# Five edits to the token mixing of a decoder block: gating's product on another engine, three projection tiles at once, the norm's end in single tiles, triangles turned later

## The chip, the core and the metric

The kernel runs on one core of a Trainium2 chip, in one launch. The metric is the device time in microseconds; a run's time is that of its one core. Three runs of the kernel before took 1669.92 to 1671.87 us, with a median of 1670.35.

## What is computed

The reference is one layer of a hybrid decoder block on 1024 positions of width 1024, all in float32. It has three parts, each with an RMS norm before and after it and a residual:

- token mixing: h = norm(x), then one projection of h gives u and v (1024 columns each, GELU), the input of a diagonal state-space branch S5 (512) and two gates (1024 each);
- attention into a memory of 256 positions;
- a SwiGLU network with 2816 hidden columns.

The change is in the token mixing, and in the norm of the memory at the start. What matters of it, cut from the reference:

```python
y   = rms_norm(mem, g_mem)                                 # 256 x 1024, at the kernel's start
u, v = split(gelu(z_gm)); v = layer_norm(v)
w   = where(tril, w_s, 0)                                  # 8 triangles of 128 x 128
sv  = einsum('gts,bnsgc->bntgc', w, v) + b_s               # per chunk of 128 positions
y_gm = u * sv                                              # the gating
y_s5 = y * sigmoid(y @ w_glu)                              # end of S5, 512 channels
merged = sigmoid(z_ga) * (y_gm @ w_br_gm) + sigmoid(z_gb) * (y_s5 @ w_br_s5)
```

## The kernel before, in words

**Precision.** Each operand of a large product is split into a high half (a cast to fp32r on ScalarE) and a low half (the rest, a subtraction on VectorE), and each product is three matmuls of halves (`mm3`, L521; the matmuls themselves show as L519). `put` (L527 to 530) makes such a split: the cast at L529, the subtraction at L530. Weights are loaded by SyncE's queue (`load`, L89) into three raw buffers and split into pairs (`split`, L98: cast L103, subtraction L104); SyncE asks for the next load as soon as the subtraction has freed a raw buffer. There are eight buffers of split weights and eight PSUM banks of 128x512.

**Order of the work.** The order is written out by hand: each engine runs its instructions in the order in which the program issues them, and the queue of an engine stands at an instruction that waits. Work beside the main products is put into generators by `bg(gen, delay)` (L64). `sub()` (L67) counts one turn, runs each generator that is due up to its next `yield n` (due again n turns later), in the order in which they were queued, and then lets `pump` split one weight block ahead if there is room. The product functions call `sub` once or twice to a block: `tblock` (L539) after every second of its four inner steps, `run` in `v_phase` after two of four tiles. `drain` (L79) runs the turns that are left with no matmuls between them.

**The start** (`start`, L649 on). The two memory tiles `ms` are squared and summed on ScalarE, VectorE makes the reciprocal root, `pump` splits the first weight block, then ScalarE scales the first tile (L667) and VectorE the second (L668). Then both are turned on TensorE (`turn`, L582).

**v and the norm** (`v_phase`, L1146 on). v's eight tiles of 128 positions come from products with the operands "11", "T1", ... "T4" in two sets of four banks, X and Y. `ln(half)` (L1153) is the layer norm of four tiles: four squares, one to a turn, VectorE's short operations for the reciprocal root, and at L1165 to 1170 four ACTIVATEs that apply it, two to a turn. `ln(1)` runs beside the product "21", `ln(0)` is queued after "T4" and runs beside the first blocks of `s5_out`. `wturn` (L1218) turns the eight triangles of w_s in two steps of four, each into a bank that ScalarE copies out (L1223, L1224), and then makes in two more steps the bias term, which VectorE adds to `bb`. It is queued after VectorE's sums out of the banks Y, ahead of "T4".

**S5's output** (`s5_out`, L1060 on). Four glu tiles, each in two halves: product, sigmoid on ScalarE (L1076), product on VectorE, split. Then the projection by channels to 1024 columns: eight blocks `m` of two halves, each times the gate read back from DRAM (`gb`). Blocks 0 and 1 are done at once in four banks: first the inner steps 0 to 2 of all four tiles, nine matmuls each, then the last step of all four. That way the fourth glu tile is wanted later. Blocks 2 to 7 follow one by one, twelve matmuls a half.

**The gating** (`gm_gen`, L1259 on) is queued ahead of the projection with a delay of 3 and runs beside it: 16 steps (8 groups, two halves), one every second turn. A step is eight short matmuls, VectorE's scale and bias out of the bank (stt), the product with u (`self.tt`, u loaded from DRAM by SyncE one group ahead, L1267), and `put` for the split that the merge multiplies with. `merge` (L1291 on) begins with `drain`; its first block takes the low and high halves of the eight groups in turn.

Of the kernel before, what the change touches and what calls it, by code (L numbers as in the profile page):

```python
# [14 lines left out]
ALU = mybir.AluOpType  # L15
# [21 lines left out]
class Builder:  # L37
# [480 lines left out]
    def mm(self, ps, a, b, start, stop, more=False):  # L518
        self.nc.tensor.matmul(ps, a, b, start=start, stop=stop, skip_group_check=more)  # L519
# [129 lines left out]
    def start(self):  # L649

        nc, i = self.nc, self.ins
        mem, x = i["mem"][0], i["x"][0]
        self.kvd = self.dr.tile([4, P, 1024], F, name="kvd", tag="kvd")
        ms = [self.slot() for _ in range(2)]
        for t, m in enumerate(ms):
            nc.sync.dma_start(m, mem[t * 128:t * 128 + 128])
        self.consts()
        self.load()
        xs = [self.slot() for _ in range(8)]
        lx = lambda half: [nc.sync.dma_start(xs[t], x[t * 128:t * 128 + 128]) for t in range(4 * half, 4 * half + 4)]  # L660
        lx(0)
        st = self.newst()
        for t, m in enumerate(ms):
            self.square(m, st[:, t:t + 1])
        r = self.rms(st, 2)
        self.pump()
        nc.scalar.mul(ms[0], ms[0], r[:, 0:1])  # L667
        self.ts(ms[1], ms[1], r[:, 1:2], ALU.mult)  # L668
        mt = [self.pair(), self.pair()]
        mv = lambda k: tuple(s[:, (k % 4) * 256:(k % 4) * 256 + 256] for s in mt[k // 4])  # L670
        for _ in self.turn(ms, 3, mv):
            pass
        ms = None
        self.hT = [self.pair() for _ in range(8)]
        hs = self.hs = lambda half: lambda k: tuple(s[:, half * 512:half * 512 + 512] for s in self.hT[k])

        def xgen():
            for half in range(2):
                st = self.newst()
                for t in range(4):  # L680
                    self.square(xs[4 * half + t], st[:, t:t + 1])
                    yield 1
                if not half:
                    lx(1)
                r = self.rms(st, 4)
                for t in range(4):
                    self.ts(xs[4 * half + t], xs[4 * half + t], r[:, t:t + 1], ALU.mult)
                yield 4
                yield from self.turn(xs[4 * half:4 * half + 4], 0, hs(half))
                for t in range(4):  # L690
                    xs[4 * half + t] = None
            self.xok = True
            self.s5_load()
            self.bg(self.s5_gen(), 5)
            self.bg(self.h_sums(), 8)
        self.bg(xgen())
        for c in range(2):
            ks = self.slot()
            for m in range(4 * c, 4 * c + 4):
                if m % 2 == 0:  # L700
                    ps = self.bank()
                w = self.get(("k", m))
                self.tblock(ps[:, (m % 2) * 256:(m % 2) * 256 + 256], w, 0, mv, every=4)
                self.rel()
                if m % 2:
                    nc.scalar.copy(ks[:, (m % 4 - 1) * 256:(m % 4 + 1) * 256], ps)
            nc.scalar.dma_start(self.kvd[c], ks)
        vs = [self.slot(), self.slot()]
        for cb in range(2):
            pss = [self.bank(), self.bank()]  # L710
            for kp in range(4):
                w = self.get(("kv", cb, kp))
                self.nblock(pss, w, 2 * kp, lambda k, t: tuple(s[:, t * 128:t * 128 + 128] for s in mv(k)), kp == 3)
                self.rel()
            for t in range(2):
                nc.scalar.copy(vs[t][:, cb * 512:cb * 512 + 512], pss[t])
        for t in range(2):
            nc.scalar.dma_start(self.kvd[2 + t], vs[t])
# [341 lines left out]
    def s5_out(self):  # L1060
        nc = self.nc
        while len(self.yT) < 4 or not self.yok:
            self.sub()
        yT, self.yT = self.yT, None
        yr, self.yr = self.yr, None
        ys = []
        for m in range(4):
            if m % 2 == 0:
                w = self.get(("glu", m // 2))
            y = self.pair()  # L1070
            t = self.slot()
            for half in range(2):
                o = slice(half * 512, half * 512 + 512)
                ps = self.bank()
                self.tblock(ps, w, (m % 2) * 128, lambda k: tuple(s[:, o] for s in yT[k]), 4)
                nc.scalar.activation(out=t[:, o], in_=ps, func=AF.Sigmoid)  # L1076
                self.tt(t[:, o], t[:, o], yr[m][:, o], ALU.mult)
                self.put(tuple(s[:, o] for s in y), t[:, o])
            ys.append(y)
            if m % 2:  # L1080
                self.rel()
        yT = yr = None
        gb = {}

        def lg(m):
            gb[m] = self.slot()
            nc.sync.dma_start(gb[m], self.gd["gb"][m])
        lg(0)
        lg(1)
        self.bg(self.gm_gen(), 3)  # L1090
        late = []
        w = self.get(("bs", 0))

        tiles = [(m, half, self.bank()) for m in range(2) for half in range(2)]
        for ks in (range(3), range(3, 4)):
            for m, half, ps in tiles:
                for k in ks:
                    self.mm3(ps, tuple(x[:, k, m * 128:m * 128 + 128] for x in w),
                             tuple(s[:, half * 512:half * 512 + 512] for s in ys[k]), k == 0, k == 3)
                self.sub()  # L1100
                if ks[0]:
                    o = slice(half * 512, half * 512 + 512)
                    self.tt(gb[m][:, o], ps, gb[m][:, o], ALU.mult)
        tiles = ps = None
        self.rel()
        late += [(self.gd["mb"][m], gb.pop(m)) for m in range(2)]
        lg(2)
        for m in range(2, 8):
            if m < 7:
                lg(m + 1)  # L1110
            if m % 2 == 0:
                w = self.get(("bs", m // 2))
            g = gb.pop(m)
            for half in range(2):
                o = slice(half * 512, half * 512 + 512)
                ps = self.bank()
                self.tblock(ps, w, (m % 2) * 128, lambda k: tuple(s[:, o] for s in ys[k]), 4)
                self.tt(g[:, o], ps, g[:, o], ALU.mult)
            if m % 2:
                self.rel()  # L1120
            while late:
                nc.scalar.dma_start(*late.pop(0))
            late.append((self.gd["mb"][m], g))
        nc.scalar.dma_start(*late.pop(0))
# [21 lines left out]
    def v_phase(self, fin):  # L1146

        nc, i = self.nc, self.ins
# [4 lines left out]
        def ln(half):  # L1153
            st = sums[half]
            mu = st[:, 40:44]
            self.tt(mu, st[:, 32:36], st[:, 36:40], ALU.add)
            self.ts(mu, mu, -1.0 / D, ALU.mult)
            for t in range(4):
                j = self.jk.tile([P, 1024], BF, name="jk", tag="jk", bufs=1)
                nc.scalar.activation(out=j, in_=vt[4 * half + t], func=AF.Square, bias=mu[:, t:t + 1],  # L1160
                                     accum_out=st[:, t:t + 1])
                yield 1
            yield from self.rms_slow(st, 4)
            self.tt(st[:, 48:52], mu, st[:, 16:20], ALU.mult)
            for t in range(4):  # L1165
                v = vt[4 * half + t]
                nc.scalar.activation(out=v, in_=v, func=AF.Identity, scale=st[:, 16 + t:17 + t], bias=st[:, 48 + t:49 + t])  # L1167
                if t % 2:
                    yield 1
            if not half:  # L1170
                self.vok = True
        X, Y = ([self.bank() for _ in range(4)] for _ in range(2))
# [37 lines left out]
        w = self.slot()  # L1210
# [36 lines left out]
            self.tt(vt[t][:, h0], Y[t], vt[t][:, h0], ALU.add)  # L1247
            gelu(vt[t][:, h0], vt[t][:, h0], st(0, 0, t))
        Y = None
        self.bg(wturn(), 2)  # L1250
        run(X, "T4", False)
        del self.fxs["T4"]
        self.hT = None
# [5 lines left out]
    def gm_gen(self):  # L1259
        nc, i = self.nc, self.ins  # L1260
# [10 lines left out]
        for g in range(8):  # L1271
            y = self.pair()
            lu(g + 1)
            u = us.pop(g)
            for half in range(2):
                o = slice(half * 512, half * 512 + 512)
                ps = self.bank()
                for n in range(4):
                    self.mm(ps[:, n * 128:n * 128 + 128], self.vt[4 * half + n][:, g * 128:g * 128 + 128],
                            self.wt[:, g * 128:g * 128 + 128], True, True)  # L1280
                t = self.tmp()
                self.stt(t.rearrange("p (n t) -> p n t", n=4), ps.rearrange("p (n t) -> p n t", n=4), self.gc[:, 32 + g:33 + g],
                         self.bb[:, g * 128:g * 128 + 128].unsqueeze(1).to_broadcast([P, 4, 128]), ALU.mult, ALU.add)
                self.tt(u[:, o], t, u[:, o], ALU.mult)
                self.put(tuple(s[:, o] for s in y), u[:, o])
                yield 2
            self.ygm[g] = y
            u = y = t = ps = None
# [675 lines left out]
```

## Time and profile before

| what | value |
|---|---|
| median of three runs | 1670.35 us |
| the profiled execution's own time | 1670.15 us |
| its span in the profile | 1668.4 us |
| mean granted clock of TensorE | 0.994 |
| busy: TensorE, VectorE, ScalarE, GpSimd | 1628.1, 1150.6, 681.7, 102.7 us |

The span is what the profile shows from the first to the last instruction; about 1.75 us of the execution's time lie around it. A busy TensorE is not TensorE at its peak, since matmuls are pipelined, but a wait of TensorE shows as a gap. In a timeline, the bracket at the end of a row is the idle time of that engine just before the instruction and what ended it. The granted clock of a stretch is given as a share of 2.4 GHz.

### The profile page before, as it was taken

The numbers are of one execution on the slowest core, as the hardware profiler recorded it, in microseconds if no ns is written. First come the engines' busy times: TensorE is split into PE (matmuls) and PEld (weight loads), VectorE is DVE, ScalarE is ACT, GpSimd is POOL, SyncE is SP. The second block draws the span as 40 slices with busy tenths as digits, with TensorE's granted clock in tenths as the row PEclk, the third lists the DMA queues.
The fourth block names the chain that finished last, engine by engine and source line by source line (L and its number), as shares of the span: only waits on it lengthen the run. The fifth ranks groups of instructions, "written<-read, shape, count | busy, mean of one in ns | idle before, by whom it ended". The sixth has DMA issues, their size and how long they took to land.

```text
span 1668.4 us, 20995 instructions
## 1 busy us (share of the span) xinstructions
PE 1628.1 (98%) x7788; PEld 1364.4 (82%) x7788; DVE 1150.6 (69%) x2053; ACT 681.7 (41%) x1196; POOL 102.7 (6%) x97
## 2 busy tenths in 40 slices
PE   7999989999999999999999999999999999999997
PEld 7898878887887778888888888888888888888886
DVE  5679788967444674447864577687778777666778
ACT  6642212135457222235543447753233223245454
POOL 0025500012500000000000000000000000000000
PEclk9999999999999999999999999999999999999999
DMA  8669922245231474444523153673545446463634
GB/s 278 207 122 200 234 74 90 76 134 186 113 113 51 163 283 158 141 147 143 172 69 125 53 192 112 216 244 130 180 139 173 149 158 202 142 225 132 226 112 161
DMA packets 223414, 259.53 MB, mean 156 GB/s; under 512 B 14824, under 2 KB 157200, under 8 KB 223120
## 3 DMA queue, kind: packets, MB, share of 16 engines
q1 hardware_dynamic: 176208, 181.24, 33.7%
q10 hardware_dynamic: 26496, 60.18, 9.7%
q0 software_dynamic: 20608, 16.78, 5.9%
q8 instruction: 61, 1.00, 0.2%
q14 instruction: 41, 0.34, 0.1%
HBM read 183.31 MB, written 77.33 MB: 156 GB/s over the span
## 4 chain that ended last, share of the span: by engine, by line
PE 83%; DVE 7%; ACT 5%; issue 2%; DMA 2%; SPq 0%; ACTq 0%; DVEq 0%
PE ps L519 79%; DVE act L134 2%; DVE ws L104 1%; ACT jk L575 1%; DVE ws L134 1%; ACT ws L103 1%; DMA wr<-in_ca_w_kv_dram 1%; ACT act L529 1%; DVE act L530 1%; DVE act L140 1%; PE ps L587 1%; ACT jk L1160 1%; DMA wr<-actd 1%; PE ps L508 1%; ACT act L1167 0%
## 5 line engine op out<-in xcount | busy, mean ns | idle before, releaser
L519 PE MATMUL ps<-act,ws 128*128 128x512 f32 (+1 forms) x4212 | 970.1, 388 | 9.6 <-ACT act L529 7.3
L519 PEld LDWEIGHTS ps<-act,ws 128*128 128x128 f32 x4212 | 775.4, 189 | 165.9 <-ACT act L529 8.1
L519 PE MATMUL ps<-ws,act 128*128 128x512 f32 x1392 | 332.8, 395 | 0.0
L519 PEld LDWEIGHTS ps<-ws,act 128*128 128x128 f32 x1392 | 270.2, 208 | 45.0
L134 DVE TENSOR_TENSOR act<-act 128x512 f32<-128x512 f32 (+6 forms) x521 | 287.3, 580 | 15.2 <-ACT act L1076 8.0
L519 PE MATMUL ps<-ws 128*128 128x512 f32 x852 | 193.3, 389 | 0.0
L519 PEld LDWEIGHTS ps<-ws 128*128 128x128 f32 x852 | 159.9, 188 | 33.2
L104 DVE TENSOR_TENSOR ws<-wr,ws 128x1024 fp32r<-128x1024 f32 x100 | 122.1, 1223 | 93.3 <-ACT ws L103 93.1
L134 DVE TENSOR_TENSOR act<-ps,act 128x512 f32<-128x512 f32 x201 | 135.6, 683 | 43.5 <-PE ps L519 34.1
L134 DVE TENSOR_TENSOR ws<-act,ws 128x512 fp32r<-128x512 f32 x107 | 74.0, 692 | 88.9 <-ACT ws L1754 51.8
L134 DVE TENSOR_TENSOR ws<-tm,ws 128x512 fp32r<-128x512 f32 x108 | 78.2, 724 | 79.4 <-ACT ws L1547 58.9
L1547 ACT CAST ws<-tm 128x512 fp32r<-128x512 f32 x88 | 54.8, 622 | 168.8 <-PE ps L519 111.5
L103 ACT CAST ws<-wr 128x1024 fp32r<-128x1024 f32 x100 | 104.7, 1047 | 42.8 <-PE ps L519 29.3
L134 DVE TENSOR_TENSOR ws<-wr,ws 128x512 fp32r<-128x512 f32 x130 | 91.7, 706 | 28.2 <-ACT ws L1547 14.9
L529 ACT CAST act<-act 128x512 fp32r<-128x512 f32 (+1 forms) x92 | 57.5, 637 | 129.5 <-DVE act L134 117.1
L530 DVE TENSOR_TENSOR act<-act 128x512 fp32r<-128x512 f32 (+1 forms) x92 | 65.3, 720 | 46.1 <-ACT act L529 46.1
L519 PE MATMUL ps<-act 128*128 128x256 f32 (+2 forms) x504 | 86.6, 317 | 0.2
L519 PEld LDWEIGHTS ps<-act 128*128 128x128 f32 x504 | 74.7, 190 | 9.6 <-DVE act L134 0.8
L1754 ACT CAST ws<-act 128x512 fp32r<-128x512 f32 x71 | 44.2, 622 | 89.6 <-PE ps L519 48.3
L1831 POOL DMA_DIRECT2D out_dram<-act x4 | 2.2, 561 | 1171.8 <-DVE act L134 1171.8
L530 DVE TENSOR_TENSOR act<-ps,act 128x512 fp32r<-128x512 f32 x48 | 32.5, 687 | 39.7 <-ACT act L529 39.7
L890 ACT ACTIVATE act<-ps 128x512 f32<-128x512 f32 x32 | 19.2, 600 | 80.4 <-PE ps L519 46.6
(164 smaller groups left out, 1112.5 us busy)
## 6 DMA issues: line engine op xcount, KB each, us to landing
wr<-in_ffn_w_gu_dram SPq DMA_DIRECT2D x39, 512.0 KB, 4.2
actd<-act ACTq DMA_DIRECT2D x77, 256.0 KB, 2.2
wr<-actd SPq DMA_DIRECT2D x38, 512.0 KB, 3.7
wr<-in_w_in_dram SPq DMA_DIRECT2D x28, 512.0 KB, 3.9
act<-in_ffn_w_gu_dram SPq DMA_DIRECT2D x22, 512.0 KB, 5.1
act<-in_ffn_w_down_dram SPq DMA_DIRECT2D x44, 256.0 KB, 4.3
td<-act POOLq DMA_DIRECT2D x40, 256.0 KB, 6.6
pd<-act ACTq DMA_DIRECT2D x17, 512.0 KB, 4.4
```

What stands on the lines that cost most here:

```text
L103: self.nc.scalar.copy(hi, t)
L104: self.nc.vector.tensor_tensor(out=lo, in0=t, in1=hi.bitcast(F), op=ALU.subtract)
L134: self.nc.vector.tensor_tensor(out=out, in0=a, in1=b, op=op)
L140: self.nc.vector.scalar_tensor_tensor(out=out, in0=a, scalar=s, in1=b, op0=op0, op1=op1)
L508: nc.tensor.matmul(py[:, o], self.rr[:, 512 + i * 128:640 + i * 128], cc[:, 512 + i * 128:640 + i * 128], start=False, stop=True)
L519: self.nc.tensor.matmul(ps, a, b, start=start, stop=stop, skip_group_check=more)
L529: self.nc.scalar.copy(dst[0], src)
L530: self.nc.vector.tensor_tensor(out=dst[1], in0=src, in1=dst[0].bitcast(F), op=ALU.subtract)
L575: self.nc.scalar.activation(out=j[:, 0:n], in_=src, func=AF.Square, accum_out=col)
L890: nc.scalar.activation(out=g[:, half * 512:half * 512 + 512], in_=ps, func=AF.Sigmoid)
L1547: self.nc.scalar.copy(t[:, 0:512], now)
L1754: nc.scalar.copy(w[:, h[0]], src)
```

## The change

Five edits:

- In `start`, VectorE's scaling of the second memory tile is issued first, then ScalarE's of the first, and the split of the weight block (`pump`) after both.
- In `s5_out`, blocks 0 to 2 are done at once in six banks instead of 0 and 1 in four; both weight pairs are fetched and three gates asked for ahead. The gating is queued with a delay of 6 instead of 3.
- In `ln`, each of the four last ACTIVATEs has a turn of its own.
- In `v_phase`, `wturn` is queued with a delay of 5 instead of 2.
- In `gm_gen`, the product with u is issued to GpSimd (`self.gt`, L136 to 137) instead of VectorE.

```diff
@@ -663,9 +663,9 @@
         for t, m in enumerate(ms):
             self.square(m, st[:, t:t + 1])
         r = self.rms(st, 2)
+        self.ts(ms[1], ms[1], r[:, 1:2], ALU.mult)
+        nc.scalar.mul(ms[0], ms[0], r[:, 0:1])
         self.pump()
-        nc.scalar.mul(ms[0], ms[0], r[:, 0:1])
-        self.ts(ms[1], ms[1], r[:, 1:2], ALU.mult)
         mt = [self.pair(), self.pair()]
         mv = lambda k: tuple(s[:, (k % 4) * 256:(k % 4) * 256 + 256] for s in mt[k // 4])
         for _ in self.turn(ms, 3, mv):
@@ -1087,15 +1087,16 @@
             nc.sync.dma_start(gb[m], self.gd["gb"][m])
         lg(0)
         lg(1)
-        self.bg(self.gm_gen(), 3)
+        self.bg(self.gm_gen(), 6)
         late = []
-        w = self.get(("bs", 0))
-
-        tiles = [(m, half, self.bank()) for m in range(2) for half in range(2)]
+        ws = [self.get(("bs", 0)), self.get(("bs", 1))]
+
+        lg(2)
+        tiles = [(m, half, self.bank()) for m in range(3) for half in range(2)]
         for ks in (range(3), range(3, 4)):
             for m, half, ps in tiles:
                 for k in ks:
-                    self.mm3(ps, tuple(x[:, k, m * 128:m * 128 + 128] for x in w),
+                    self.mm3(ps, tuple(x[:, k, m % 2 * 128:m % 2 * 128 + 128] for x in ws[m // 2]),
                              tuple(s[:, half * 512:half * 512 + 512] for s in ys[k]), k == 0, k == 3)
                 self.sub()
                 if ks[0]:
@@ -1103,9 +1104,10 @@
                     self.tt(gb[m][:, o], ps, gb[m][:, o], ALU.mult)
         tiles = ps = None
         self.rel()
-        late += [(self.gd["mb"][m], gb.pop(m)) for m in range(2)]
-        lg(2)
-        for m in range(2, 8):
+        w = ws[1]
+        late += [(self.gd["mb"][m], gb.pop(m)) for m in range(3)]
+        lg(3)
+        for m in range(3, 8):
             if m < 7:
                 lg(m + 1)
             if m % 2 == 0:
@@ -1165,8 +1167,7 @@
             for t in range(4):
                 v = vt[4 * half + t]
                 nc.scalar.activation(out=v, in_=v, func=AF.Identity, scale=st[:, 16 + t:17 + t], bias=st[:, 48 + t:49 + t])
-                if t % 2:
-                    yield 1
+                yield 1
             if not half:
                 self.vok = True
         X, Y = ([self.bank() for _ in range(4)] for _ in range(2))
@@ -1247,7 +1248,7 @@
             self.tt(vt[t][:, h0], Y[t], vt[t][:, h0], ALU.add)
             gelu(vt[t][:, h0], vt[t][:, h0], st(0, 0, t))
         Y = None
-        self.bg(wturn(), 2)
+        self.bg(wturn(), 5)
         run(X, "T4", False)
         del self.fxs["T4"]
         self.hT = None
@@ -1281,7 +1282,7 @@
                 t = self.tmp()
                 self.stt(t.rearrange("p (n t) -> p n t", n=4), ps.rearrange("p (n t) -> p n t", n=4), self.gc[:, 32 + g:33 + g],
                          self.bb[:, g * 128:g * 128 + 128].unsqueeze(1).to_broadcast([P, 4, 128]), ALU.mult, ALU.add)
-                self.tt(u[:, o], t, u[:, o], ALU.mult)
+                self.gt(u[:, o], t, u[:, o], ALU.mult)
                 self.put(tuple(s[:, o] for s in y), u[:, o])
                 yield 2
             self.ygm[g] = y
```

## Rows read from the trace of the kernel before

**Rows 1.** The page: the first line of its busy times (share of the span, number of instructions), and the chain that ended last by engine.

```profile
PE 1628.1 (98%) x7788; PEld 1364.4 (82%) x7788; DVE 1150.6 (69%) x2053; ACT 681.7 (41%) x1196; POOL 102.7 (6%) x97
...
PE 83%; DVE 7%; ACT 5%; issue 2%; DMA 2%; SPq 0%; ACTq 0%; DVEq 0%
```

**Rows 2.** What TensorE waited for in the whole run: instruction <- releaser: us in total, times, longest in us.

```profile
PE ps L519 <- ACT act L529: 7.3, 2, 3.7
...
PE ps L587 <- ACT act L667: 3.5, 1, 3.5
...
PE ps L1223 <- DVE act L134: 3.3, 1, 3.3
```

**Rows 3.** Slices of 2 us: the slice, its length and TensorE's busy time in it (instructions), granted clock as a share of 2.4 GHz, DMA share, GB/s.

```profile
550.00:552.00 2.00, 2.00 (x6) 0.50 0.94 343
...
552.00:554.00 2.00, 2.00 (x9) 0.83 0.22 88
...
620.00:622.00 2.00, 2.00 (x8) 0.76 0.08 29
```

**Rows 4.** Timeline of the start: start us, length us, engine, line, operation, out<-in, count [idle of the engine before it <- releaser].

```profile
9.41 1.23 DVE L104 TENSOR_TENSOR ws<-wr,ws 128x1024 fp32r<-128x1024 f32 x1
...
9.52 1.15 ACT L667 ACTIVATE act<-act,st 128x1024 f32<-128x1024 f32 x1 [0.68 <-DVE st L140]
...
10.55 0.75 DVE L144 TENSOR_SCALAR act<-act,st 128x1024 f32<-128x1024 f32 x1
...
11.36 3.46 PE L587 MATMUL ps<-ident,act 128*128 128x128 f32 x15 [0.16 <-DVE act L144]
...
11.87 3.46 ACT L533 ACTIVATE act<-ps,gc 128x256 fp32r<-128x256 f32 x8 [1.20 <-PE ps L587]
...
20.24 1.03 ACT L103 CAST ws<-wr 128x1024 fp32r<-128x1024 f32 x1
```

**Rows 5.** Timeline from 509 us to the first wait in S5's projection by channels, columns as in the last group.

```profile
509.11 2.48 DVE L134 TENSOR_TENSOR act<-ps,act 128x512 f32<-128x512 f32 x4
...
509.23 4.64 ACT L1167 ACTIVATE act<-act,st 128x1024 f32<-128x1024 f32 x4 [2.75 <-DVE st L134]
...
521.97 1.15 ACT L1160 ACTIVATE jk<-act,st 128x1024 bf16<-128x1024 f32 x1 [0.49 <-DVE st L144]
...
526.25 17.94 PE L519 MATMUL ps<-act,ws 128*128 128x512 f32 x78
...
537.74 4.64 ACT L1167 ACTIVATE act<-act,st 128x1024 f32<-128x1024 f32 x4 [1.43 <-DVE st L134]
...
547.08 0.62 ACT L529 CAST act<-act 128x512 fp32r<-128x512 f32 x1 [1.40 <-DVE act L134]
...
547.75 0.50 PE L519 MATMUL ps<-act,ws 128*128 128x512 f32 x1 [3.56 <-ACT act L529]
```

**Rows 6.** Timeline of the projection with the gating, and of the merge's beginning, columns as before.

```profile
554.76 1.05 PE L519 MATMUL ps<-act 128*128 128x128 f32 x8
...
555.86 0.75 DVE L140 SCALAR_TENSOR_TENSOR tm<-ps,gc,act 128x512 f32<-128x512 f32 x1
...
561.66 0.69 DVE L134 TENSOR_TENSOR act<-tm,act 128x512 f32<-128x512 f32 x1 [5.06 <-DMA act<-ud]
...
599.92 1.05 PE L519 MATMUL ps<-act 128*128 128x128 f32 x8
...
603.55 1.05 PE L519 MATMUL ps<-act 128*128 128x128 f32 x8
...
604.61 1.23 DVE L104 TENSOR_TENSOR ws<-wr,ws 128x1024 fp32r<-128x1024 f32 x1 [0.26 <-ACT ws L103]
...
606.62 5.02 PE L519 MATMUL ps<-act,ws 128*128 128x512 f32 x21
...
609.76 0.74 DVE L140 SCALAR_TENSOR_TENSOR tm<-ps,gc,act 128x512 f32<-128x512 f32 x1
...
610.53 0.69 DVE L134 TENSOR_TENSOR act<-tm,act 128x512 f32<-128x512 f32 x1
...
611.26 0.62 ACT L529 CAST act<-act 128x512 fp32r<-128x512 f32 x1 [2.74 <-DVE act L134]
...
613.12 0.74 DVE L140 SCALAR_TENSOR_TENSOR tm<-ps,gc,act 128x512 f32<-128x512 f32 x1
...
615.33 9.88 PE L519 MATMUL ps<-act,ws 128*128 128x512 f32 x30 [3.69 <-ACT act L529]
```

**Rows 7.** GpSimd's tensor operations of line 137: two of the eight forms that the view of this line lists (count: shortest/median/longest in ns, first and last start, shapes); then timeline rows of 366 to 440 us, columns as before.

```profile
L137 POOL TENSOR_TENSOR tm<-wr,act x6: 1287/1292/1697, 372.9 to 421.5; 128x512 f32<-128x512 f32 x6
...
L137 POOL TENSOR_TENSOR tm<-wr,tm x3: 1294/1606/2210, 371.2 to 405.0; 128x512 f32<-128x512 f32 x3
...
366.37 1.61 POOL L137 TENSOR_TENSOR tm<-tm,wr 128x512 f32<-128x512 f32 x1 [10.15 <-issue]
...
368.01 0.62 ACT L925 CAST ws<-tm 128x512 fp32r<-128x512 f32 x1 [5.19 <-POOL tm L137]
...
409.46 0.69 DVE L134 TENSOR_TENSOR ws<-tm,ws 128x512 fp32r<-128x512 f32 x1 [2.08 <-ACT ws L925]
...
410.30 1.29 POOL L137 TENSOR_TENSOR tm<-wr,act 128x512 f32<-128x512 f32 x1 [4.00 <-DVE ws L134]
...
439.38 1.59 DVE L134 TENSOR_TENSOR ws<-tm,ws 128x512 fp32r<-128x512 f32 x1 [0.76 <-ACT ws L925]
```

## The prediction

> **What bounds the kernel now.** The page comes first: TensorE is busy for 98% of the span, and the chain that ended last is 83% TensorE [rows 1]. So a part of the change gains only where TensorE waits, and loses where it makes TensorE wait. The list of TensorE's waits says where that is [rows 2]. Three lines touch the change: 3.5 us at the start for ScalarE's half of the norm (L667), 3.3 us for a bank when the triangles are turned (L1223), and two waits for ScalarE's cast of a split (L529), 7.3 us together. The timelines place these two: one within S5's projection by channels, over at 547.75 [rows 5], one before the merge's last operand, over at 615.33 [rows 6]. The granted clock, in slices of 2 us, shows what else they cost: after the first it is still 0.50 (1.2 GHz) at 550 and back within the slice from 552, after the second it is back only in that from 620 [rows 3]. That is 4 and 6 us at half speed, so 2 and 3 us lost.
>
> The last wait decides, and it has to be read back. TensorE had all gating matmuls done at 606.62 and 21 matmuls of the merge left that need no more; then it needed the high half of the eighth gating tile, which VectorE and ScalarE had not made: the step whose matmuls begin at 603.55 and last about a microsecond is taken up by VectorE at 613.12, 8.5 us late [rows 6]. A step on VectorE is a fixed sequence in program order: scale and bias out of the bank (stt, 609.76), product with u (610.53), wait for ScalarE's cast (611.26), low half, one product of S5's projection with its gate, next stt (613.12): 3.36 us. TensorE's own period is 3.63 (599.92 to 603.55). VectorE is late nevertheless, because three weight splits fall in the stretch, 1.23 us each behind a wait of 0.26 (604.61), and because its first product stood 5.06 us for the load of u, until 561.66.
>
> **The change part by part.** A "turn" below is one of the calls at which queued background work runs, one or two to a block of matmuls.
>
> *Product on GpSimd.* The product leaves VectorE, but the low half that follows it in VectorE's order subtracts the cast of that very product. VectorE has nothing to run meanwhile: its queue stands at the subtract until GpSimd and then ScalarE are done, and the next gate product, the next stt and each weight split are queued behind it. What counts is the length of this loop, not VectorE's busy time. Today it is 0.73 from the product's start to that of the cast (610.53 to 611.26) [rows 6]. On GpSimd a 128x512 product takes 1.29 (median of the first form; of the other 1.61, longest 2.21) [rows 7]. GpSimd starts 0.15 after VectorE's result is there (409.46 + 0.69 to 410.30), where VectorE itself goes on after 0.03 (609.76 + 0.74 to 610.53); ScalarE follows it by 0.03 (366.37 + 1.61 to 368.01). I take 0.08 for the extra hand-over, between 0 and that 0.12: 0.08 + 1.29 + 0.03 = 1.40, so +0.67 a step; the bounds are +0.6 and, with 1.61, +1.0. I take 1.29 because the longer ones stand where VectorE worked beside GpSimd, and here it waits. The period becomes 4.03, above TensorE's 3.63: the stretch is bound by this loop.
>
> The Trainium skill speaks against the move: "GPSIMD Engine Reference", section 3.1, gives GpSimd 1.96 times VectorE's time for an elementwise operation of two inputs, 4497 ns at 2048 elements. Scaled to 512 that is an estimate of 1.12 us, by which a step would grow by 0.50 and the sum below be 2.5 us smaller; the row's 1.29 is the higher.
>
> *Three blocks at once, gating from the sixth turn.* The first gating matmuls come after six tiles of nine matmuls instead of three, 27 matmuls later. Today they start at 554.76 [rows 6]. At 0.23 a matmul (78 in 17.94) [rows 5] the 27 cost 6.2, so they start at 561.0 if TensorE resumes as now, the stt at 562.1 (1.10 later, as 554.76 to 555.86), the first product 0.85 after that, at 563.0 instead of 561.66: +1.3. The load of u is then no longer late; VectorE waits for TensorE in its place. The projection still has 32 turns (12 + 20 instead of 8 + 24), but gating, 16 steps two turns apart, now ends at turn 36 instead of 33: two steps instead of one fall into the drain, where TensorE has no projection to run. Before the fifteenth product VectorE has 16 gate products to do instead of 15: +0.6. The three weight splits fall on turns without gating, where the cast can be done ahead: I take off 0.8 (3 x 0.26). Nothing for the third gate load on SP (it stands ahead of the load of u, which has time now), for the second pair of weights (split before the projection in either order), or for six banks held: gating takes the two left in turn, and the stt that frees each is over when TensorE wants it.
>
> *Triangles later.* The two turnings go from the 2nd and 6th turn of the product T4 to the 5th turn and the first of the glu blocks. By then 18 more matmuls have run on banks that TensorE holds, and VectorE's four sums of 509.11 are over: the 3.3 us go. What is late next is ScalarE, which works almost without a gap from 509.23 [rows 5]. TensorE, now at 544.19 (526.25 + 17.94), would be there at 540.9, and waits for the cast of the third glu tile (547.08) all the same. I count the gain at nothing, the cover being that this cast comes no earlier.
>
> *A tile a turn in the norm.* Four ACTIVATEs of 4.64 us in a row (537.74) become two and two around a glu block. The tile between comes 2.3 earlier, but the one that TensorE waits for stands behind all four as before. Two terms are left: the second triangle's copy moves into a gap of ScalarE, 0.49 before 521.97: -0.5; and the two sums for the bias (0.62 each, as 509.11) now stand among VectorE's short operations for the second norm and delay its first ACTIVATE by 1.3, of which 0.4 comes back as the weight split is out of the way of the third tile's product: +0.9. Net +0.4, bounds -0.7 and +1.2. It goes through to gating.
>
> *Start.* VectorE's half of the norm goes ahead of the weight split (10.55 to about 9.5), so the second tile's transposes no longer wait (11.36 to about 10.9) [rows 4]. ScalarE's cast of these weights moves behind its own half, 9.52 + 1.1, and ends at about 11.65, when the first scaled copy can run instead of at 11.87. VectorE's split ends at 12.9 instead of 10.64; the fourth weight load, which SP asks for when it ends, goes 2.3 later, and its cast is at 20.24: 7 us of cover are left. Gain 0.2, bounds 0 and 0.5.
>
> **Sum**, at the time at which the merge goes on: 1.3 (first product) + 0.4 (norm) + 14 x 0.67 = 9.4 + 0.6 - 0.8 + 0.7 (the fifteenth product itself) = 11.6, so 626.9 instead of 615.33. Less 0.2 at the start: 11.4. The profiled execution took 1670.15 (span 1668.4 and 1.75 around it), 0.2 under the median of 1670.35, so 1681.6. I let the clock fall after both waits as now; the rest is bound by TensorE and only moves.
>
> **Rivals.** *VectorE is relieved* (chance 0.10): if the products that leave it were what held it up, the loop would fall below TensorE's 3.63, the merge would not wait, and 3.7 us with 3 us of clock come back: 1663.5. It decides if VectorE can go on to the next gate product before the low half. For it: VectorE is late by 8.5 us. Against it: VectorE stands for the cast in every step now, and nothing passes. *Shared access* (0.10): GpSimd's 1.61 or more at all 15, with VectorE at its side (at 439.38 a subtract of VectorE took 1.59 beside GpSimd, 0.69 elsewhere) [rows 7]: +5, 1686.5. Against it: the two take turns here. The Trainium skill's "GPSIMD Engine Reference", section 8, has the two share their interfaces to SBUF; that row agrees. *The turning pays* (0.10): ScalarE's chain is not what sets 547.75, TensorE resumes 2 to 3 us sooner and the clock stays up once: 1676 to 1679. *It cancels* (0.05): that, the start and a loop without growth: within 0.2%. My forecast has 0.65.
>
> The range runs from 1675.5, the forecast with the turning and without one of the clock's falls, to 1687.5, the forecast with shared access and the norm's upper bound. Slower 0.85, same 0.05, faster 0.10; 0.2% is about what a measurement of this kernel can tell from no change.
>
> **What would show it.** Right: 16 more products of about 1.3 us on GpSimd; VectorE's stt 4.0 apart; no wait at L1223, but some 7 us in the projection, over near 548; the wait before the merge over near 627. Wrong: stt 3.4 to 3.6 apart and no wait before the merge (VectorE relieved); the projection's wait over before 546 (the turning pays).

## The result and the profile after

The changed kernel takes 1679.9 us (median of 4 runs, 1678.7 to 1682.0); the kernel before took 1671.1 beside it (median of 4, 1669.9 to 1672.1). The ratio is 1.0054, with a 95% interval of 1.0037 to 1.0072: slower by 8.8 us, between 6 and 12. The forecast was 1681.6, within 1675.5 to 1687.5, and slower.

The page of the changed kernel comes first: its busy times, and the chain that ended last by engine.

```profile
PE 1629.5 (97%) x7788; PEld 1363.6 (81%) x7788; DVE 1140.1 (68%) x2037; ACT 681.4 (41%) x1196; POOL 122.5 (7%) x113
...
PE 57%; DVE 3%; ACT 1%; issue 1%; DMA 1%; POOL 0%; DVEq 0%; ACTq 0%; SPq 0%; POOLq 0%
```

Against [rows 1], VectorE does 10.5 us less work in 16 instructions fewer and GpSimd 19.8 more in 16 more; TensorE's busy time is the same to 1.4 us. Read as shares, the change relieves the second busiest engine. The time went up although VectorE's work went down, so the busy shares decide nothing here. (The shares of the chain add up to 63%: it was followed back over the later part of the span only, and is not compared with [rows 1].) TensorE's waits say more (instruction, releaser, us in total, times, longest):

```profile
PE ps L519 <- ACT act L529: 15.0, 3, 7.1
...
PE ps L587 <- ACT act L667: 3.5, 1, 3.5
PE ps L519 <- DVE act L134: 3.1, 3, 2.2
...
PE ps L519 <- DVE tm L140: 1.6, 2, 0.9
```

Against [rows 2], the 3.3 us for a bank at the turning are gone, and the waits for ScalarE's cast went from 7.3 to 15.0. TensorE also stands for banks that VectorE frees too late (L134 and L140; 4.1 of these in four waits between 593 and 614). By this reading that costs nothing more, since the merge waits for the end of the same work on VectorE. The timeline says where those are. First the norm and the start of the projection (L1169 is the norm's last ACTIVATE, L1167 before; L1224 the turning).

```profile
507.18 0.38 DVE L146 TENSOR_SCALAR st<-st 128x4 f32<-128x4 f32 x2 [0.37 <-ACT jk L1162]
...
510.72 2.48 DVE L134 TENSOR_TENSOR act<-ps,act 128x512 f32<-128x512 f32 x4
510.84 2.38 ACT L1169 ACTIVATE act<-act,st 128x1024 f32<-128x1024 f32 x2 [2.75 <-DVE st L134]
...
512.17 0.60 PE L1224 MATMUL ps<-ident,act 128*128 128x128 f32 x4
...
540.06 2.38 ACT L1169 ACTIVATE act<-act,st 128x1024 f32<-128x1024 f32 x2 [2.02 <-DVE st L134]
...
544.20 1.24 ACT L1169 ACTIVATE act<-act,st 128x1024 f32<-128x1024 f32 x1
...
546.27 1.24 ACT L1169 ACTIVATE act<-act,st 128x1024 f32<-128x1024 f32 x1
...
548.75 0.62 ACT L529 CAST act<-act 128x512 fp32r<-128x512 f32 x1 [0.76 <-DVE act L134]
...
549.42 13.45 PE L519 MATMUL ps<-act,ws 128*128 128x512 f32 x48 [7.12 <-ACT act L529]
```

The turning has no wait, the four ACTIVATEs of the second norm are two and two around a glu block (between 544.20 and 546.27 a cast of a weight split comes in), and TensorE stands 7.12 at 549.42 where it stood 3.56 [rows 5]: the 3.3 us moved there. The first row is where this document starts to count time. It is the first of VectorE's short operations behind the four squares of the first norm, just ahead of the changed stretch; it came at 505.57 before, so 1.61 of the profiled run's delay was already there, from stretches that no edit touches apart from the start. All stage times below are counted from this row of each kernel (the *marker*).

Then the gating, of which one whole step and the end are shown.

```profile
562.71 1.05 PE L519 MATMUL ps<-act 128*128 128x128 f32 x8
...
563.80 0.75 DVE L140 SCALAR_TENSOR_TENSOR tm<-ps,gc,act 128x512 f32<-128x512 f32 x1 [6.28 <-PE ps L519]
564.63 1.28 POOL L137 TENSOR_TENSOR act<-tm,act 128x512 f32<-128x512 f32 x1 [103.94 <-DVE tm L140]
...
588.40 1.64 ACTq L1124 DMA_DIRECT2D mbd<-act  x3
...
590.14 1.05 ACT L103 CAST ws<-wr 128x1024 fp32r<-128x1024 f32 x1 [1.18 <-issue]
...
591.23 1.23 DVE L104 TENSOR_TENSOR ws<-wr,ws 128x1024 fp32r<-128x1024 f32 x1 [0.94 <-ACT ws L103]
...
600.44 0.74 DVE L140 SCALAR_TENSOR_TENSOR tm<-ps,gc,act 128x512 f32<-128x512 f32 x1
...
601.32 1.28 POOL L137 TENSOR_TENSOR act<-tm,act 128x512 f32<-128x512 f32 x1 [2.77 <-DVE tm L140]
...
602.63 0.62 ACT L529 CAST act<-act 128x512 fp32r<-128x512 f32 x1 [3.43 <-POOL act L137]
603.28 0.69 DVE L530 TENSOR_TENSOR act<-act 128x512 fp32r<-128x512 f32 x1 [2.10 <-ACT act L529]
603.89 0.68 DVE L134 TENSOR_TENSOR act<-ps,act 128x512 f32<-128x512 f32 x1
604.50 0.74 DVE L140 SCALAR_TENSOR_TENSOR tm<-ps,gc,act 128x512 f32<-128x512 f32 x1
...
626.46 1.26 POOL L137 TENSOR_TENSOR act<-tm,act 128x512 f32<-128x512 f32 x1 [2.71 <-DVE tm L140]
627.75 0.62 ACT L529 CAST act<-act 128x512 fp32r<-128x512 f32 x1 [3.36 <-POOL act L137]
...
628.42 4.08 PE L519 MATMUL ps<-act,ws 128*128 128x512 f32 x8 [6.49 <-ACT act L529]
```

The step reads as a ring: stt at 600.44, GpSimd's product, ScalarE's cast, VectorE's low half after 2.10 us of standing, the gate product, the next stt at 604.50. From stt to stt it is 4.06, where it was 3.36 [rows 6], and nothing in it overlaps anything else of it. Before, VectorE stood for the cast as well, but shorter:

```profile
611.91 0.69 DVE L530 TENSOR_TENSOR act<-act 128x512 fp32r<-128x512 f32 x1 [0.69 <-ACT act L529]
```

So in a step VectorE is spared a product of 0.69 and stands 2.10 instead of 0.69, 1.41 longer. The merge goes on at 628.42, 121.24 after the marker; before, 109.76 after it.

The granted clock follows (slice of 2 us, its length, busy time of TensorE, of its weight loads, VectorE, ScalarE and GpSimd, granted clock, DMA share, GB/s).

```profile
548.00:550.00 2.00, 0.58 (x1) 0.29 (x1) 1.29 (x2) 1.11 (x2) 0.00 (x0) 0.50 0.52 157
...
554.00:556.00 2.00, 2.00 (x10) 1.62 (x10) 1.31 (x3) 1.31 (x2) 0.00 (x0) 1.00 0.59 231
...
622.00:624.00 2.00, 0.00 (x0) 0.00 (x0) 0.41 (x1) 0.22 (x1) 1.26 (x1) 0.55 0.35 141
...
630.00:632.00 2.00, 2.00 (x6) 1.52 (x6) 0.20 (x1) 0.85 (x2) 1.11 (x1) 0.50 0.00 0
632.00:634.00 2.00, 2.00 (x9) 1.60 (x8) 1.75 (x3) 0.71 (x1) 0.00 (x0) 0.89 0.00 0
```

It falls at both waits, as before [rows 3]. The second time it falls early in the slice from 622, with no matmul in that slice and 6 us before TensorE goes on (before, it fell early in the slice from 614, at 0.53, about 1 us before TensorE went on), so much of the half speed passes while TensorE stands; after 628.42 TensorE works 4.0 us at it (to 632.44, if the 0.89 is a slice that began at 0.50), where it was 5.6 before (615.33 to 620.96, by the 0.76 of [rows 3] in the same way).

### The profile page after: what moved, and what is told of

It reads as the page before. It is cut to its first block, busy times and chain, and to the rows that moved or that the text cites. A ratio compares the mean times of both kernels' runs of the same rounds, so it can differ in the third digit from the quotient of the medians.

```text
span 1680.3 us, 21019 instructions
## 1 busy us (share of the span) xinstructions
PE 1629.5 (97%) x7788; PEld 1363.6 (81%) x7788; DVE 1140.1 (68%) x2037; ACT 681.4 (41%) x1196; POOL 122.5 (7%) x113
## 4 chain that ended last, share of the span: by engine, by line
PE 57%; DVE 3%; ACT 1%; issue 1%; DMA 1%; POOL 0%; DVEq 0%; ACTq 0%; SPq 0%; POOLq 0%
PE ps L519 55%; DVE act L134 1%; DVE act L140 1%; DMA wr<-actd 1%; DVE ws L134 1%; ACT jk L575 0%; DVE ws L104 0%; PE ps L1469 0%; PE ps L1423 0%; PE ps L587 0%; DMA act<-mbd 0%; DVE act L530 0%; DVE st L140 0%; POOL act L137 0%; ACT act L529 0%
## 5 line engine op out<-in xcount | busy, mean ns | idle before, releaser
L134 DVE TENSOR_TENSOR act<-act 128x512 f32<-128x512 f32 (+6 forms) x521 | 287.5, 581 | 14.5 <-ACT act L1076 7.4
L134 DVE TENSOR_TENSOR act<-ps,act 128x512 f32<-128x512 f32 x201 | 135.8, 684 | 42.6 <-PE ps L519 33.2
L134 DVE TENSOR_TENSOR ws<-act,ws 128x512 fp32r<-128x512 f32 x107 | 73.9, 691 | 88.5 <-ACT ws L1755 51.8
L134 DVE TENSOR_TENSOR ws<-tm,ws 128x512 fp32r<-128x512 f32 x108 | 78.2, 725 | 78.9 <-ACT ws L1548 58.5
L530 DVE TENSOR_TENSOR act<-act 128x512 fp32r<-128x512 f32 (+1 forms) x92 | 66.5, 732 | 68.0 <-ACT act L529 68.0
L134 DVE TENSOR_TENSOR ws<-wr,ws 128x512 fp32r<-128x512 f32 x130 | 91.1, 702 | 29.7 <-ACT ws L1548 15.4
L530 DVE TENSOR_TENSOR act<-ps,act 128x512 fp32r<-128x512 f32 x48 | 32.5, 688 | 39.7 <-ACT act L529 39.7
```

Of the source, the lines that this page charges most:

```text
L134: self.nc.vector.tensor_tensor(out=out, in0=a, in1=b, op=op)
L530: self.nc.vector.tensor_tensor(out=dst[1], in0=src, in1=dst[0].bitcast(F), op=ALU.subtract)
```

## The experiments

The theory: VectorE, GpSimd and ScalarE form a ring in VectorE's program order, and the product on GpSimd makes each turn of it 0.6 to 0.7 longer; that is nearly all of the loss. The rivals: GpSimd and VectorE slow each other (shared access), or the other four edits cost or gain something (the later first product, the turning, the norm). The table gathers what the runs gave. Times are medians; the stage times are from the marker; the kernel before took 1672.12 (13 runs) beside e1 to e4 and 1670.87 (13 runs) beside e5 to e8.

| kernel | us | ratio to before, 95% | projection resumes | first product | merge goes on [its wait] |
|---|---|---|---|---|---|
| before | | | 42.18 | 56.09 | 109.76 [3.69] |
| after | 1679.9 | 1.0037 to 1.0072 | 42.24 | 57.45 | 121.24 [6.49] |
| e1 GpSimd alone | 1681.4 | 1.0043 to 1.0077 | 42.30 | 56.03 | 119.41 [5.58] |
| e2 after, product on VectorE | 1674.1 | 1.0007 to 1.0025 | 42.25 | 57.17 | 112.91 [5.31] |
| e3 after, late split | 1664.1 | 0.9941 to 0.9971 | 42.24 | 57.81 | no wait |
| e4 before, late split | 1663.9 | 0.9938 to 0.9972 | 42.19 | 56.07 | no wait |
| e5 turning alone | 1671.7 | 0.9996 to 1.0015 | 42.89 | 56.75 | 110.53 [3.12] |
| e6 e3, norm on VectorE | 1658.9 | 0.9911 to 0.9944 | 37.92 | 52.81 | no wait |
| e7 after, gating from turn 3 | 1680.7 | 1.0041 to 1.0071 | 42.24 | 56.24 | 119.47 [5.53] |
| e8 e6, turning early | 1661.0 | 0.9924 to 0.9953 | no wait | 55.18 | no wait |

**e1: the product on GpSimd, and nothing else.**

```diff
-                self.tt(u[:, o], t, u[:, o], ALU.mult)
+                self.gt(u[:, o], t, u[:, o], ALU.mult)
```

> The kernel before with the product with u on GpSimd and nothing else. Theory (the loop of one gating step, VectorE to GpSimd to ScalarE to VectorE, is what counts): stt 4.03 us apart instead of 3.36, the first product still at about 561.7 when u has landed, so the merge goes on 15 x 0.67 = 10 us later than 615.3, at 625.4; 1680.5 us. Rival (VectorE relieved of 16 x 0.69): no wait before the merge, 1664. Rival (the loss of the whole change comes from its other edits): no difference, 1670.5.

Measured: 1681.43 (1678.88 to 1684.51), as slow as the whole change; the merge goes on 9.65 later from the marker than before. The timeline of its end, one whole step apart:

```profile
621.08 0.74 DVE L140 SCALAR_TENSOR_TENSOR tm<-ps,gc,act 128x512 f32<-128x512 f32 x1
621.90 1.26 POOL L137 TENSOR_TENSOR act<-tm,act 128x512 f32<-128x512 f32 x1 [2.72 <-DVE tm L140]
...
625.05 0.74 DVE L140 SCALAR_TENSOR_TENSOR tm<-ps,gc,act 128x512 f32<-128x512 f32 x1
...
627.84 4.51 PE L519 MATMUL ps<-act,ws 128*128 128x512 f32 x9 [5.58 <-ACT act L529]
```

The stt are 3.97 apart, the product is 1.26. By the times, this one edit accounts for the loss (9.3 above before; the whole change 8.8). The traces tell the two apart: here the merge goes on 1.83 sooner from the marker than in the whole change, and from the marker to the end the run is 1.05 shorter; the medians don't show a difference of that size.

**e2: the other four edits** (after, with the edit of e1 taken back).

> The kernel after with the product with u back on VectorE; the four other edits stay. Theory: stt 3.36 us apart again; the gating begins 1.4 us later than in the kernel before (27 matmuls more ahead of it against the load of u), has one more gate product ahead of the last step, and its three weight splits cost 0.3 less each: the merge goes on 1 to 2 us later than before; 1671 to 1672 us. Rival (the other edits pay, the turning's 3.3 us above all): 1667.

Measured: 1674.11 (1671.82 to 1677.2, 10 runs), 2.0 above before, so these four together cost rather than pay. The merge goes on 3.15 later from the marker, and the time is 2 us longer, both more than was expected. The first product is 1.08 later; the rest is in the loop, above all in one step with a weight split (6.89 from product to product, where such a step took 4.85):

```profile
587.05 3.06 ACTq L1124 DMA_DIRECT2D mbd<-act  x3
...
590.21 1.05 ACT L103 CAST ws<-wr 128x1024 fp32r<-128x1024 f32 x1 [2.55 <-issue]
...
591.29 1.23 DVE L104 TENSOR_TENSOR ws<-wr,ws 128x1024 fp32r<-128x1024 f32 x1 [2.30 <-ACT ws L103]
```

With three blocks done at once, their three stores are issued together on ScalarE's queue, ahead of the cast that the split needs: VectorE stands 2.30 where it stood 0.26 [rows 6]. (In after the same stores took 1.64 to issue and VectorE stood 0.94; in the kernel before two stores were issued together, in 0.82 from 578.00, with no split right behind them.) This is read off the traces; no run moves the stores. It is also why e1 and e2 don't add up: at the merge they give 9.65 and 3.15, the whole change 11.48, and that step is 2.04 longer than before in e2, but 0.74 longer in after than a step with a split in e1 (5.49, the shortest of its three).

**e3: after, with the split one step late.** The cast and the low half of a product are issued behind the next step's product, so VectorE has an stt and a gate product to do while GpSimd and ScalarE work.

```diff
+        held = []
...
                 self.gt(u[:, o], t, u[:, o], ALU.mult)
-                self.put(tuple(s[:, o] for s in y), u[:, o])
+                for x in held:
+                    self.put(*x)
+                held = [(tuple(s[:, o] for s in y), u[:, o])]
...
+        self.put(*held.pop())
```

> The kernel after with the product on GpSimd, but the split of a gating step (ScalarE's cast and VectorE's low half) is issued one step later, behind the next step's stt and product. Theory: VectorE and ScalarE no longer stand for GpSimd, a step costs VectorE 0.6 + 0.7 + 0.6 = 2.0 us of work, TensorE's period of 3.63 sets the pace, and no wait of TensorE before the merge is left: some 14.5 us of waiting and 2 us of half clock less than in the kernel after, 1663 us. Rival (GpSimd's 1.29 us or access to SBUF shared with VectorE sets the pace, now that both work at once): stt still 4 us apart or products of 1.6 us and more, 1675 to 1680.

Measured: 1664.06 (1663.46 to 1665.18), 15.8 under after, 8 under before. A step of the timeline:

```profile
599.96 0.75 DVE L140 SCALAR_TENSOR_TENSOR tm<-ps,gc,act 128x512 f32<-128x512 f32 x1 [1.68 <-PE ps L519]
...
600.62 0.68 DVE L530 TENSOR_TENSOR act<-act 128x512 fp32r<-128x512 f32 x1
600.79 1.67 POOL L137 TENSOR_TENSOR act<-tm,act 128x512 f32<-128x512 f32 x1 [1.96 <-DVE tm L140]
601.22 0.68 DVE L134 TENSOR_TENSOR act<-ps,act 128x512 f32<-128x512 f32 x1
...
602.49 0.62 ACT L529 CAST act<-act 128x512 fp32r<-128x512 f32 x1 [3.01 <-POOL act L137]
...
603.58 0.75 DVE L140 SCALAR_TENSOR_TENSOR tm<-ps,gc,act 128x512 f32<-128x512 f32 x1 [1.68 <-PE ps L519]
```

VectorE now waits for TensorE (1.68 for the bank), the stt are 3.62 apart, TensorE's own pace, and the merge doesn't wait. GpSimd's product got slower, 1.67 instead of 1.28, where one of VectorE's low halves (L530) runs beside it, and it costs nothing.

**e4: the kernel before, with the split one step late** (the same edit, product on VectorE).

> The kernel before, product on VectorE, with the split of a gating step issued one step later. Theory: the 0.73 us for which VectorE stands for the cast in every step goes, a step costs it 2.7 us with the product, less than TensorE's 3.63; the wait of 3.7 us before the merge and the 3 us of half clock after it go: 1664 us. Rival (it is VectorE's work, with the weight splits, and not the standing that made it late): the wait remains, 1669 to 1670.

Measured: 1663.94 (1663.54 to 1664.18), the same as e3. TensorE's waits:

```profile
PE ps L519 <- ACT act L529: 3.6, 1, 3.6
...
PE ps L1223 <- DVE act L134: 3.3, 1, 3.3
```

The wait before the merge is gone without GpSimd. What held VectorE up before was the standing in its order, not the work; once that is out of the way, the five edits together are worth nothing (1664.06 with them, 1663.94 without). What GpSimd's product is worth by itself there is not shown: the late split with only the four other edits was not run.

**e5: the later turning alone** (in the kernel before).

```diff
-        self.bg(wturn(), 2)
+        self.bg(wturn(), 5)
```

> The kernel before with the triangles turned from the 5th turn instead of the 2nd and nothing else. Theory (ScalarE's chain of glu tiles ends last there): the wait of 3.3 us at the turning goes, the wait in the projection by channels grows by as much, from 3.6 to about 7, and TensorE goes on there at the same time within 1 us; 1670 to 1672 us, no gain. Rival (the turning pays): TensorE goes on 3.3 us sooner, 1667 to 1668.

Measured: 1671.71 (1668.0 to 1673.76, 10 runs), no difference. The wait at the turning is gone, and the one in the projection is 7.77 instead of 3.56 [rows 5]:

```profile
551.23 7.85 PE L519 MATMUL ps<-act,ws 128*128 128x512 f32 x21 [7.77 <-ACT act L529]
```

It ends 0.7 later from the marker. The 3.3 us were covered by ScalarE's chain, as the prediction had it.

**e6: e3, with the norm's last operation on VectorE**, to see whether ScalarE's chain is what sets that wait.

```diff
-                nc.scalar.activation(out=v, in_=v, func=AF.Identity, scale=st[:, 16 + t:17 + t], bias=st[:, 48 + t:49 + t])
+                self.ts(v, v, st[:, 16 + t:17 + t], ALU.mult, st[:, 48 + t:49 + t], ALU.add)
```

> The kernel with the late split (other four edits and GpSimd's product in), and in addition the norm's eight last operations on VectorE (one multiply and add of 128x1024 each, 0.75 us as the scaling at the start) instead of ScalarE's ACTIVATE of 1.16. Theory (ScalarE's chain sets the wait of 7.1 us in the projection): ScalarE loses 9.3 us of work ahead of the third glu tile, VectorE has room for its 6 us; TensorE's wait falls from 7.1 to 2 us or less and with it 2 us of half clock: 1655 to 1658 us. Rival (the wait is set by VectorE's short operations or TensorE's own order): 1662 to 1664.

Measured: 1658.87 (1658.4 to 1661.03), 12.0 under the kernel before beside it, where e3 was 8.1 under its own, and the fastest of all; about 1 us short of what was expected.

```profile
509.79 1.54 DVE L146 TENSOR_SCALAR act<-act,st 128x1024 f32<-128x1024 f32 x2
...
544.06 0.51 PE L519 MATMUL ps<-act,ws 128*128 128x512 f32 x1 [1.80 <-ACT act L529]
```

The projection resumes 4.3 sooner from the marker, and TensorE waits 1.80 there instead of 7.12.

**e7: after, with the gating from the third turn**, as before.

```diff
-        self.bg(self.gm_gen(), 6)
+        self.bg(self.gm_gen(), 3)
```

> The kernel after with the gating queued with a delay of 3 again; three blocks at once and all else stay. Theory: gating begins when u has landed, 1.3 us sooner, one step more is covered by the projection, and one gate product fewer stands ahead of the fifteenth step, so the merge goes on 1.3 to 2.5 us sooner than in the kernel after; 1677.5 to 1679 us. Rival (the later beginning keeps VectorE's lag small and helps): no difference or slower, 1680 or more.

Measured: 1680.71 (1680.02 to 1682.13): the time shows no gain over after, against the expectation, and lies where the rival put it. In the trace the first product is 1.2 sooner and the merge goes on 1.8 sooner, after a wait of 5.53. Part of that is given back: after it TensorE works 6.1 us at half speed (625.15 to 631.2, by the slice below, columns as above), where it was 4.0 in after, so from the marker to the end the run is only 0.5 shorter.

```profile
630.00:632.00 2.00, 2.00 (x8) 1.59 (x7) 1.90 (x3) 0.03 (x1) 0.00 (x0) 0.70 0.00 0
```

An effect of this size is not told apart by these times, so the price of the later gating rests on the traces alone.

**e8: e6, with the turning early again.** If ScalarE's chain was the cover of the turning's wait, the later turning must pay once that chain is short.

> The kernel with late split and norm on VectorE, with the triangles turned from the 2nd turn again. Theory: with ScalarE's chain out of the way TensorE's own path counts, and the turning's wait for a bank, which cost nothing as long as ScalarE was last, now costs 2 to 3.3 us against the same kernel with the later turning: 1658 to 1660 us. Rival (the turning never costs anything): the same time as that kernel.

Measured: 1661.04 (1660.12 to 1663.17), 2.2 above e6, each about 1 us above what was expected. Four times each, with ranges that overlap, are few for 2.2 us, but from the marker to the end the two traces differ by 2.2 as well. TensorE waits at the turning, and not in the projection:

```profile
511.54 1.09 PE L1224 MATMUL ps<-ident,act 128*128 128x128 f32 x4 [4.87 <-DVE act L134]
```

So the edit that gives nothing in the kernel before (e5) gives about 2 us where its cover is gone.

## Why the prediction was right

**The sum held, and so did its main term; two smaller terms did not.** It is made at the merge's going on, 11.48 later from the marker than before; predicted 11.6 (without the start).

| term | predicted | measured |
|---|---|---|
| first product, with the norm | 1.3 + 0.4 | 1.36 |
| 14 turns of the ring | 14 x 0.67 = 9.4 | 14 x 0.636 = 8.9 |
| one more gate product | 0.6 | 0.6 |
| three splits with their casts ahead | -0.8 | +0.1 |
| the fifteenth product | 0.7 | 0.52 |

That the total came out within 0.1 is in part luck: the splits cost 0.9 more than predicted, and the ring, the norm and the fifteenth product together 1.0 less.

- *The ring.* From the first product to the fifteenth went 52.23 before and 61.83 after, in fourteen steps: one that has a gate product more now, three with a split, and ten plain ones, which took 34.92 together and take 41.28, 0.64 more each. The three with a split grew by 2.02, 0.1 more than three times 0.64. The price of 1.29 was right (1.26 to 1.29 in all 16), because the two engines take turns, as argued. By the Trainium skill's "GPSIMD Engine Reference", section 3.1, the estimate was 1.12; no product of the changed kernel is that short. e1 shows that the edit carries the whole loss, e4 that VectorE's work was not what held it up.
- *First product.* TensorE needed 13.29 from resuming to the first gating matmul, where it needed 7.01: 6.28 more, against the 6.2 for 27 matmuls. The load of u was no longer late.
- *Norm.* The step failed in size: net +0.06 (42.18 to 42.24) instead of +0.4, inside its bounds.
- *Splits.* This step failed. Two of the three did save 0.3 (5.14 and 5.19 for a step with a split, where a plain one and a split side by side would make 5.49, the 4.85 of before and 0.64), but the third took 6.23, because VectorE stood 0.94 for its cast. The three stores that finish together on ScalarE's queue were not counted among what that edit moves. Without the GpSimd edit VectorE stood 2.30 there (e2).
- *Turning.* Counted at nothing, with ScalarE's chain as cover: e5 shows no gain, e6 and e8 that the cover is what was named.
- *Start.* TensorE's first product came 0.46 sooner (14.01, before 14.47), and the gain is not to be seen later: TensorE then waits 0.52 for the next weight split, and the norm's marker is 1.61 later than before in the profiled run.

```profile
14.01 3.63 PE L519 MATMUL ps<-act,ws 128*128 128x256 f32 x26
...
18.16 7.09 PE L519 MATMUL ps<-act,ws 128*128 128x256 f32 x57 [0.52 <-DVE ws L104]
```

- *The clock.* "I let the clock fall after both waits as now" was a little too high: the 5.6 us at half speed after the merge's wait became 4.0, which gives 0.8 back. From the marker to the end the profiled run is 10.3 longer, 1.2 less than at the merge.

The profiled run of after (1682.04) is the slowest of its four, and 11.9 over that of before: 1.6 from ahead of the stage, 10.3 from it. The medians differ by 8.8, with an interval that holds 10.3. What the rest of that spread is stays open: the marker lies between 505.6 and 510.0 in these ten kernels, also where nothing ahead of it was changed.

**The rivals.** *VectorE is relieved* needed VectorE to go on before the low half. In the change it can't, and its stt are 4.0 apart in a plain step. In e3 it can, and the time is 1664.06, where that rival gave 1663.5; but e4 has the same time without GpSimd, so the order alone is enough to give it. *Shared access* is real in e3 (1.28 becomes 1.67; the Trainium skill's "GPSIMD Engine Reference", section 8, agrees) and absent from the change, in which the engines wait for each other. *The turning pays* fell with e5.

## What to carry to other kernels

When engines hand a tile on in a ring and one of them comes back to it in program order, add up the ring, not the busy times: moving one link to a slower engine lengthens every turn, however much work it takes off the busier one. The remedy is in the order: put the part that waits one step later, behind work that is ready. Before a wait is removed, find which engine's chain ends next, for the edit pays only after that one has been shortened (nothing in e5, about 2 us between e8 and e6).

## What the runs showed of the hardware that was not expected

- In e3 the one of GpSimd and VectorE that began later was the one that took longer. The 13 products of 128x512 that began while a low half of VectorE (L530) ran took 1.61 to 1.74 us, the other three 1.27 to 1.29, as in the change. A low half that began while a product ran took 1.40 where it takes 0.69, and weight splits 1.49 to 1.72 where they take 1.23. VectorE's gate product (L134), which reads PSUM, ran beside the first product (564.98 to 566.25) and did not slow it.

```profile
609.95 1.29 POOL L137 TENSOR_TENSOR act<-tm,act 128x512 f32<-128x512 f32 x1 [0.24 <-issue]
610.40 1.40 DVE L530 TENSOR_TENSOR act<-act 128x512 fp32r<-128x512 f32 x1 [0.58 <-ACT act L529]
```

- Scale and bias of a 128x1024 f32 tile in place took 0.80 to 0.82 on VectorE (e6) and 1.23 to 1.24 on ScalarE (before).
- A longer wait need not cost more clock: with 6.49 us of standing in place of 3.69, TensorE did less of its work at 0.50 after it (4.0 against 5.6 us), since the low clock began 6 us before it went on. The length of the wait alone does not tell it: after 5.53 us (e7) it was 6.1.
